# Pairing the first activations with the first weights in the input DMAs of a two-layer encoder kernel

## The chip, the cores and the metric

The kernel runs on one core of a Trainium2 chip. The metric is the device time of one execution in microseconds (us). Work on the core is shared by five engines, each with its own queue that it works through in order: PE (TensorE, matrix products), DVE (VectorE), ACT (ScalarE), POOL (GpSimd) and SP (SyncE, which here only issues DMAs). DMAs move data between the chip's main memory (HBM) and the on-chip memory that the engines read; a DMA's data may be used when all of it has landed.

## The reference

The reference is a hybrid encoder trunk of two layers on 512 tokens of width 1024. Cut to what matters here, a layer is

```python
for i in range(DEPTH):                       # DEPTH = 2
    h = _mixer_sublayer(x, ...)              # begins with proj = x @ w_in[i], 1024 -> 5120 columns
    x = _layer_norm(DEEPNORM_ALPHA * x + h, ln1_g[i], ln1_b[i])
    mlp = jnp.square(jax.nn.relu(x @ w_up[i])) @ w_down[i]
    gate = jax.nn.sigmoid(x @ w_ple_gate[i] + b_ple_gate[i])
    x = _layer_norm(DEEPNORM_ALPHA * x + mlp + gate * (p[i] @ w_ple[i]), ln2_g[i], ln2_b[i])
```

The mixer splits `proj` into queries, keys and values of two kinds of attention (windowed, with shared keys; and dilated in three groups) and into the logits of two gates, and joins the two attentions by those gates. All inputs are float32. What is computed first, and what this case is about, is the product of x with the first columns of `w_in` of layer 0.

## The kernel before

**Precision.** Every large product is made from three: a float32 operand is split into a rounded high part and the rest (`split`, line 248: ACT casts the high part, DVE subtracts it from the source for the low part), and `mm3` (line 306) sums high x high (line 308), x-low x w-high (309) and x-high x w-low (310) in one bank of PSUM. So a tile of x or of weights is usable by PE only after a DMA, an ACT cast and, for the low part, a DVE subtraction.

**Weights.** `plan_layer` lists weight tiles in the order of use, 128 partitions by 1024 columns (512 KB) each; `pack_weights` lays them behind one another in the array `wst`. `fetch` (line 271) issues the DMA of tile c on SP into a buffer `wst` (three buffers in turn); `prep` (line 280) splits it into `whi` and `wlo` (three buffers each as well). A weight in the list `LATER` takes another way, `split_later` (line 252): ACT writes the high part and its negative, and a DMA of POOL adds the source to that (`accum_op`). Tile 5, the first gate's weights `("g", 0, 0)`, is the first of these. `ahead` decides when tiles are fetched and prepared, two ahead of their use.

**The start.** Line 364 to 376 load x, transposed, as eight tiles of 128 rows of contraction by 512 tokens (256 KB each): `xs0` to `xs7`, rows of 2 KB out of `xT`, whose rows are 16 KB long. Tile 0 of the weights is cut into three DMAs of 128, 384 and 512 columns, fetched after `xs0`; tile 1 is fetched after `xs1`, tiles 2 and 3 after `xs7`. The first product, `linear_k_outer` (line 329), runs over contraction outside and over four output blocks m inside: weight tile j holds contraction steps k = 2j and 2j + 1, with four blocks of 128 columns each. For k = 0 it needs `xs0` and columns 0 to 511 of weight tile 0; for k = 1 `xs1` and columns 512 to 1023. Each k is 12 products of PE (four blocks, three products each), 96 in all. Before them PE runs 11 small products (`warm`, line 243) that need no input.

**The channel vectors.** For each layer a DMA of ACT's queue (line 1197) loads 40 columns of biases and norm parameters into `vraw`, and DVE halves 16 of them into `vhalf` (line 1199). The first user of `vhalf` is the first gate.

**What sets the order.** A scheduler orders each engine's queue ahead of time, from the data each instruction needs and an estimate of times; inside `manual_schedule` PE's order is that of the code. A DMA issue of SP also waits until one of eight completion counters is free, so that a ninth DMA waits for the first one to land.

Of the kernel before, what the change touches and what calls it, by code (L numbers as in the profile page):

```python
# [19 lines left out]
SP = mybir.EngineType.SP  # L20

P = 128
S = 512
D = 1024
KT = 8
DEPTH = 2
# [193 lines left out]

def build(nc, tc, plan, down, xT, xN, pT, wst, vec, rows, sink, cst, out):
    ctx = ExitStack()
    PSUM = bass.MemoryType.PSUM
    SWAP = list(range(8, 16)) + list(range(8)) + list(range(16, 32))
    with ctx:
        cp = ctx.enter_context(tc.tile_pool(name="cp", bufs=1))
        wp = ctx.enter_context(tc.tile_pool(name="wp", bufs=3))
# [18 lines left out]
        def split(hi, lo, src):  # L248
            nc.scalar.copy(hi, src)  # L249
            nc.vector.tensor_tensor(lo, src, hi.bitcast(F32), ALU.subtract)  # L250
# [7 lines left out]
        def recent(engine):  # L258
            return next(i for i in reversed(nc.cur_bb.bb.instructions) if i.engine == engine)
# [3 lines left out]
            return tc.issue_after(recent(SP)) if l else ExitStack()  # L263


        offs = np.cumsum([0] + [len(t) * P * P for _, t in plan + down])
        down_at = {key: int(offs[len(plan) + n]) for n, (key, _) in enumerate(down)}
        ready, fetched, held_sets = {}, {}, {}
        at = [0, 0, 0]

        def fetch(c):
            n = len(plan[c][1]) * P
            st = wp.tile([P, 1024], F32, tag="wst", name=f"wst{c}")
            src = wst[int(offs[c]):int(offs[c + 1])].rearrange("(p n) -> p n", p=P)
            cuts = [slice(0, n)] if c else [slice(0, P), slice(P, n // 2), slice(n // 2, n)]
            for a in cuts:
                nc.sync.dma_start(st[:, a], src[:, a])
            fetched[c] = st, cuts

        def prep(c):  # L280
            st, cuts = fetched.pop(c)
            pool, tag, bufs = held_sets.get(plan[c][0][1][0], (wp, "w", 3))
            hi, lo = (pool.tile([P, 1024], F32R, tag=tag + e, name=f"{tag}{e}{c}", bufs=bufs) for e in ("hi", "lo"))
            for a in cuts:
                (split_later if plan[c][0] in LATER else split)(hi[:, a], lo[:, a], st[:, a])
            ready[c] = (hi, lo)

        def ahead(last, further=0):
            while at[1] < len(plan) and at[1] <= max(last, further):
                fetch(at[1])  # L290
                at[1] += 1
                if at[1] - 1 <= last:
                    prep(at[2])
                    at[2] += 1
            while at[2] < len(plan) and at[2] <= last:
                prep(at[2])
                at[2] += 1
# [63 lines left out]
            return pss  # L361


        xhi = cp.tile([P, KT, S], F32R, name="xhi")
# [12 lines left out]


        def attention_block(l, av, rp, vt, OA, OB, begun):
# [813 lines left out]

        for l in range(DEPTH):
            last = l == DEPTH - 1
            vraw = cp.tile([P, 40], F32, tag="vraw", name=f"vraw{l}", bufs=2)
            nc.scalar.dma_start(vraw, vec[l])
# [26 lines left out]
            for u in range(4):  # L1224
                gs = [gate(l, 1, t, vt, np1) for t in (2 * u, 2 * u + 1)]
                w = weights((l, ("bb", u)))
# [4 lines left out]
                for n, g in enumerate(gs):  # L1231
                    t = 2 * u + n
# [313 lines left out]
```

## Time and profile before

| | us |
|---|---|
| three timed runs | 1504.95, 1506.17, 1506.33 (median 1506.17) |
| the profiled execution, its own time | 1504.93 |
| its span, first to last instruction | 1503.2 |
| PE, DVE, ACT, POOL busy | 1491.1, 1044.7, 762.4, 255.1 |
| first large product of PE starts | 4.68 |
| last of the 96 products of the start begins | 27.75 |

The page of the profile gives busy times, the chain that ended last, and the costliest groups; the trace behind it answers with a timeline of each engine. In a timeline a row is: start, duration, engine, line of the kernel, operation, written tile<-read tiles, and in brackets the idle time just before it with what ended it. "SPq", "ACTq" and "POOLq" are DMA issues on those engines' queues.

### The profile page before, as it was taken

What the parts mean: (1) busy time and instruction counts of PE and PEld (TensorE: products, weight loads), DVE (VectorE), ACT (ScalarE), POOL (GpSimd) and SP (SyncE); (2) the same over time, 40 slices, a digit from 0 to 9 for tenths busy, and PEclk for the clock granted to TensorE, in tenths of its full rate; (3) what the DMA queues carried; (4) which work ended last, traced back from release to release, by engine and by line L of the source; (5) the groups of instructions that cost most, each with busy time, mean ns of one, the idle gap of its engine ahead of it and who ended that gap; (6) DMA issues with size and microseconds to landing.
All of it is one profiled execution on the core that took longest, in us unless ns stands there. A gap on an engine that the chain in (4) does not pass through costs nothing.

```text
span 1503.2 us, 19458 instructions
## 1 busy us (share of the span) xinstructions
PE 1491.1 (99%) x7242; PEld 1241.0 (83%) x7242; DVE 1044.7 (69%) x1796; ACT 762.4 (51%) x1256; POOL 255.1 (17%) x216
## 2 busy tenths in 40 slices
PE   9999999999999999999999999999999999999997
PEld 7888888888888888888888888888888888888886
DVE  6766675458577677677877666754685867777778
ACT  5777774344344443434458777643442544444344
POOL 1212211110021110213012122102100202111121
PEclk9999999999999999999999999999999999999999
DMA  7656564555523414142366666546755233241402
GB/s 263 151 135 153 136 160 124 186 160 154 182 60 94 127 57 154 42 141 84 97 203 140 141 148 143 152 135 167 239 153 182 70 113 112 84 127 54 139 18 70
DMA packets 58894, 197.41 MB, mean 131 GB/s; under 512 B 7440, under 2 KB 7984, under 8 KB 58800
## 3 DMA queue, kind: packets, MB, share of 16 engines
q1 hardware_dynamic: 47552, 159.08, 33.1%
q0 software_dynamic: 10256, 36.70, 13.2%
q8 instruction: 56, 0.92, 0.2%
q10 hardware_dynamic: 992, 0.39, 0.1%
q14 instruction: 38, 0.31, 0.1%
HBM read 161.46 MB, written 6.37 MB: 112 GB/s over the span
## 4 chain that ended last, share of the span: by engine, by line
PE 92%; DVE 4%; ACT 1%; DMA 1%; issue 0%; POOL 0%; SPq 0%; DVEq 0%; POOLq 0%; ACTq 0%
PE dn L1156 19%; PE ps_up L310 8%; PE ps_up L309 8%; PE ps_up L308 8%; PE wo L316 2%; PE wo L314 2%; PE wo L315 2%; PE pg L314 2%; PE pg L315 2%; PE pg L316 2%; PE sa L509 1%; PE pta L472 1%; PE sb L504 1%; PE ya L308 1%; PE ya L309 1%; PE ya L310 1%
## 5 line engine op out<-in xcount | busy, mean ns | idle before, releaser
L249 ACT CAST whi<-wst 128x1024 fp32r<-128x1024 f32 (+2 forms) x120 | 121.2, 1010 | 252.2 <-PE ps_up L309 102.7
L250 DVE TENSOR_TENSOR wlo<-wst,whi 128x1024 fp32r<-128x1024 f32 (+2 forms) x120 | 149.2, 1248 | 100.8 <-ACT whi L249 99.6
L1119 POOL TENSOR_TENSOR hr<-r 128x512 f32<-128x512 f32 x64 | 108.8, 1701 | 547.4 <-ACT r L1111 516.1
L310 PE MATMUL ps_up<-xhi,wlo 128*128 128x512 f32 x512 | 199.5, 390 | 0.0
L308 PE MATMUL ps_up<-xhi,whi 128*128 128x512 f32 x512 | 199.4, 390 | 0.0
L309 PE MATMUL ps_up<-xlo,whi 128*128 128x512 f32 x512 | 199.4, 390 | 0.0
L309 PEld LDWEIGHTS ps_up<-xlo,whi 128*128 128x128 f32 x512 | 96.2, 188 | 19.9
L308 PEld LDWEIGHTS ps_up<-xhi,whi 128*128 128x128 f32 x512 | 96.1, 188 | 19.9
L310 PEld LDWEIGHTS ps_up<-xhi,wlo 128*128 128x128 f32 x512 | 96.2, 188 | 19.9
L1172 DVE TENSOR_TENSOR y<-y,dn 128x512 f32<-128x512 f32 (+1 forms) x98 | 65.9, 672 | 62.9 <-PE dn L1156 62.8
L249 ACT CAST whi<-raw 128x1024 fp32r<-128x1024 f32 x56 | 58.0, 1053 | 96.0 <-PE ps_up L309 57.7
L249 ACT CAST dhi<-raw 128x1024 fp32r<-128x1024 f32 x56 | 58.6, 1050 | 85.9 <-PE dn L1156 57.3
L256 POOL DMA_DIRECT2D wlo<-wst x54 | 47.3, 876 | 246.0 <-ACT wlo L255 151.9
L1099 DVE TENSOR_TENSOR raw<-raw,raw 128x1024 f32<-128x1024 f32 x64 | 84.7, 1324 | 0.3
L250 DVE TENSOR_TENSOR wlo<-raw,whi 128x1024 fp32r<-128x1024 f32 x56 | 68.3, 1220 | 14.1 <-ACT whi L249 14.1
L254 ACT CAST whi<-wst 128x1024 fp32r<-128x1024 f32 x54 | 56.5, 1047 | 32.3 <-PE ps_start L309 4.3
L250 DVE TENSOR_TENSOR dlo<-raw,dhi 128x1024 fp32r<-128x1024 f32 x56 | 68.9, 1239 | 3.6 <-ACT dhi L249 3.6
L255 ACT ACTIVATE wlo<-whi 128x1024 fp32r<-128x1024 f32 x54 | 57.3, 1061 | 0.9
L1156 PE MATMUL dn<-wlo,smh 128*128 128x512 f32 (+1 forms) x130 | 51.1, 393 | 0.2
L1130 DVE TENSOR_TENSOR sml<-sr,smh 128x1024 fp32r<-128x1024 f32 x32 | 43.7, 1365 | 10.8 <-ACT smh L1129 10.8
L1156 PE MATMUL dn<-whi,smh 128*128 128x512 f32 (+1 forms) x130 | 50.4, 390 | 0.0
L1156 PE MATMUL dn<-whi,sml 128*128 128x512 f32 (+1 forms) x130 | 50.3, 387 | 0.0
(860 smaller groups left out, 4039.0 us busy)
## 6 DMA issues: line engine op xcount, KB each, us to landing
wst<-wst SPq DMA_DIRECT2D x187, 512.0 KB, 3.6
raw<-wst SPq DMA_DIRECT2D x64, 512.0 KB, 4.3
wlo<-wst POOLq DMA_DIRECT2D x54, 512.0 KB, 5.0
y<-rows POOLq DMA_DIRECT2D x12, 512.0 KB, 7.0
row<-rows SPq DMA_DIRECT2D x7, 512.0 KB, 5.2
R<-line SPq DMA_DIRECT2D x24, 128.0 KB, 3.8
wst<-wst SPq DMA_DIRECT2D x9, 256.0 KB, 2.9
xs<-xT SPq DMA_DIRECT2D x8, 256.0 KB, 6.8
```

What stands on the lines that cost most here:

```text
L249: nc.scalar.copy(hi, src)
L250: nc.vector.tensor_tensor(lo, src, hi.bitcast(F32), ALU.subtract)
L308: nc.tensor.matmul(ps, w[0][:, s], x[0], start=start, stop=False, skip_group_check=part)
L309: nc.tensor.matmul(ps, w[0][:, s], x[1], start=False, stop=False, skip_group_check=part)
L310: nc.tensor.matmul(ps, w[1][:, s], x[0], start=False, stop=stop, skip_group_check=part)
L314: nc.tensor.matmul(ps, x[0], w[0][:, c], start=start, stop=False)
L315: nc.tensor.matmul(ps, x[0], w[1][:, c], start=False, stop=False)
L316: nc.tensor.matmul(ps, x[1], w[0][:, c], start=False, stop=stop)
L1099: nc.vector.tensor_tensor(to, to, other, ALU.add)
L1119: nc.gpsimd.tensor_tensor(h.rearrange("p s t -> p (s t)"), r, r, ALU.mult)
L1156: nc.tensor.matmul(ps, a[:, k, tok], w[b][:, cols], start=first and not (k or m), stop=k == 3 and m == 2, skip_group_check=True)
L1172: return nc.vector.tensor_tensor(to, to, ps, ALU.subtract if n in (2, 4, 5) else ALU.add)
```

## The change

The change touches the start and the place of two small loads; the rest of the program is the same work.

1. The host lays the first six tiles of x and the first three weight tiles side by side. `xw[k]`, for k = 0 to 5, is a block of 128 rows of 4 KB: 2 KB of x tile k, then 2 KB of the four weight blocks of that k. `xw[6]` holds x tiles 6 and 7. Tiles 0 to 2 no longer stand in `wst`.
2. `xw[0]` is loaded by three DMAs (x; 128 columns of weights; 384 columns), `xw[1]` to `xw[6]` by one DMA of 512 KB each. The tiles come from a pool of seven, all of them loaded with no wait for a buffer.
3. The split of the first weights goes in halves of 512 columns, x tile k and the weights of k one after another. For k = 0 DVE, in place of ACT, casts the first 128 columns of the weights.
4. The vectors of both layers come in one DMA, on SP behind the seven, into one tile; they are halved by one instruction.
5. Weight tiles 3, 4 and 5 are now the first to use the three `wst` buffers.

```diff
+FIRST = 3
...
-        offs = np.cumsum([0] + [len(t) * P * P for _, t in plan + down])
+        offs = np.cumsum([0] * (FIRST + 1) + [len(t) * P * P for _, t in (plan + down)[FIRST:]])
...
-            cuts = [slice(0, n)] if c else [slice(0, P), slice(P, n // 2), slice(n // 2, n)]
-            for a in cuts:
-                nc.sync.dma_start(st[:, a], src[:, a])
-            fetched[c] = st, cuts
+            nc.sync.dma_start(st[:, :n], src)
+            fetched[c] = st[:, :n]
...
+        def load_vectors():
+            with tc.issue_after(recent(SP)):
+                nc.sync.dma_start(vraws, vec)
+            nc.vector.tensor_scalar(vhs, vraws[:, :, 0:16], 0.5, None, ALU.mult)
+
...
-        with tc.tile_pool(name="xp", bufs=8) as xp:
-            for k in range(KT):
-                xs = xp.tile([P, S], F32, tag="xs", name=f"xs{k}")
-                nc.sync.dma_start(xs, xT[:, k, :])
-                if k == 0:
-                    ahead(0)
-                split(X[k][0], X[k][1], xs)
-                if k == 1:
-                    ahead(1)
+        with tc.tile_pool(name="xp", bufs=2 * FIRST + 1) as xp:
+            both = [xp.tile([P, 2 * S], F32, tag="xs", name=f"xs{k}") for k in range(2 * FIRST + 1)]
+            for k, st in enumerate(both):
+                for a in ((slice(0, S), slice(S, S + P), slice(S + P, 2 * S)) if not k else (slice(0, 2 * S),)):
+                    nc.sync.dma_start(st[:, a], xw[k][:, a])
+            load_vectors()
+            for k, st in enumerate(both):
+                if k == 2 * FIRST:
+                    for i in range(2):
+                        split(*X[k + i], st[:, i * S:(i + 1) * S])
+                    continue
+                if k % 2 == 0:
+                    ready[k // 2] = [wp.tile([P, 1024], F32R, tag="w" + e, name=f"w{e}{k // 2}", bufs=3) for e in ("hi", "lo")]
+                hi, lo = (t[:, k % 2 * S:(k % 2 + 1) * S] for t in ready[k // 2])
+                own = st[:, S:]
+                if k:
+                    split(*X[k], st[:, :S])
+                    split(hi, lo, own)
+                else:
+                    nc.vector.tensor_copy(hi[:, :P], own[:, :P])
+                    nc.scalar.copy(X[k][0], st[:, :S])
+                    nc.scalar.copy(hi[:, P:], own[:, P:])
+                    nc.vector.tensor_tensor(X[k][1], st[:, :S], X[k][0].bitcast(F32), ALU.subtract)
+                    for a in (slice(0, P), slice(P, S)):
+                        nc.vector.tensor_tensor(lo[:, a], own[:, a], hi[:, a].bitcast(F32), ALU.subtract)
+            at[1] = at[2] = FIRST
...
-            vraw = cp.tile([P, 40], F32, tag="vraw", name=f"vraw{l}", bufs=2)
-            nc.scalar.dma_start(vraw, vec[l])
-            vh = cp.tile([P, 16], F32, tag="vhalf", name=f"vhalf{l}", bufs=2)
-            nc.vector.tensor_scalar(vh, vraw[:, 0:16], 0.5, None, ALU.mult)
+            vraw, vh = vraws[:, l], vhs[:, l]
...
+    xT = np.asarray(x)[0].T.reshape(KT, P, S)
+    first = pack_weights(plan[:FIRST], big).reshape(FIRST, P, 2, S).transpose(0, 2, 1, 3).reshape(2 * FIRST, P, S)
...
+        "xw": np.ascontiguousarray(np.concatenate([np.concatenate([xT[:2 * FIRST], first], axis=2),
+                                                   np.concatenate(xT[2 * FIRST:], axis=1)[None]])),
```

SP's queue at the very start, before (`xs` are the x tiles, `wst0` and `wst1` weight tiles 0 and 1):

```order
L371 DMA xs0_89<-xT 128x512
L277 DMA wst0_91<-wst 128x128
L277 DMA wst0_91<-wst 128x384
L277 DMA wst0_91<-wst 128x512
L371 DMA xs1_105<-xT 128x512
L277 DMA wst1_109<-wst 128x1024
L371 DMA xs2_115<-xT 128x512
L371 DMA xs3_119<-xT 128x512
```

and now (`xs1` and on are the pairs, `vraw` the vectors of both layers, `ct` tables of constants):

```order
L379 DMA xs0_91<-xw 128x512
L379 DMA xs0_91<-xw 128x128
L379 DMA xs0_91<-xw 128x384
L379 DMA xs1_92<-xw 128x1024
L379 DMA xs2_93<-xw 128x1024
L379 DMA xs3_94<-xw 128x1024
L379 DMA xs4_95<-xw 128x1024
L379 DMA xs5_96<-xw 128x1024
L379 DMA xs6_97<-xw 128x1024
L368 DMA vraw_84<-vec 128x80
L276 DMA wst3_199<-wst 128x1024
L411 DMA ct0_166<-cst 128x1920
```

The first three transfers are the same sizes as before; the 512 weight columns and the x tile of k = 1, two DMAs, are one now.

ACT's queue over the same stretch, before, behind its two vector DMAs:

```order
L249 CAST xhi_84<-xs0_89 128x512
L249 CAST whi0_95<-wst0_91 128x128
L249 CAST whi0_95<-wst0_91 128x384
L249 CAST whi0_95<-wst0_91 128x512
L249 CAST xhi_84<-xs1_105 128x512
L249 CAST whi1_111<-wst1_109 128x1024
```

and now:

```order
L395 CAST xhi_86<-xs0_91 128x512
L396 CAST whi0_109<-xs0_91 128x384
L250 CAST xhi_86<-xs1_92 128x512
L250 CAST whi0_109<-xs1_92 128x512
L250 CAST xhi_86<-xs2_93 128x512
L250 CAST whi1_121<-xs2_93 128x512
```

The cast of the first 128 columns has gone to DVE, and for k = 1 the cast of the weights, which stood ahead of that of x, now stands behind it.

POOL's queue at the first gate's weights (`wlo5`, the accumulating DMA), before:

```order
L408 TENSOR_TENSOR swka0_296<-swka0_296,ct0_164 128x512
L408 TENSOR_TENSOR swqa0_0_316<-swqa0_0_316,ct0_164 128x512
L256 DMA wlo5_268<-wst5_265 128x1024
L408 TENSOR_TENSOR swqa0_1_328<-swqa0_1_328,ct0_164 128x512
L429 DMA qh0ka0_302<-qh0ka0_302 64x512
```

and now:

```order
L257 DMA wlo5_264<-wst5_261 128x1024
L432 TENSOR_TENSOR swka0_292<-swka0_292,ct0_166 128x512
L432 TENSOR_TENSOR swqa0_0_312<-swqa0_0_312,ct0_166 128x512
L453 DMA qh0ka0_298<-qh0ka0_298 64x512
L453 DMA qh1ka0_300<-qh1ka0_300 64x512
L432 TENSOR_TENSOR swqa0_1_324<-swqa0_1_324,ct0_166 128x512
```

The accumulating DMA has moved ahead of two rotary products (`swka`, `swqa`) that need results of the 96 products. Past the first score products of layer 0 the queues hold the same instructions in the same order as before.

More of the change, by code (lines that the diff above doesn't have):

```diff
@@ L219, in give, with build @@
         f[f.index(1e9)] = until
-def build(nc, tc, plan, down, xT, xN, pT, wst, vec, rows, sink, cst, out):
+def build(nc, tc, plan, down, xw, xN, pT, wst, vec, rows, sink, cst, out):
     ctx = ExitStack()
@@ L274, in fetch @@
             src = wst[int(offs[c]):int(offs[c + 1])].rearrange("(p n) -> p n", p=P)
-            cuts = [slice(0, n)] if c else [slice(0, P), slice(P, n // 2), slice(n // 2, n)]
-            for a in cuts:
-                nc.sync.dma_start(st[:, a], src[:, a])
-            fetched[c] = st, cuts
+            nc.sync.dma_start(st[:, :n], src)
+            fetched[c] = st[:, :n]
         def prep(c):
-            st, cuts = fetched.pop(c)
+            st = fetched.pop(c)
+            n = st.shape[-1]
             pool, tag, bufs = held_sets.get(plan[c][0][1][0], (wp, "w", 3))
             hi, lo = (pool.tile([P, 1024], F32R, tag=tag + e, name=f"{tag}{e}{c}", bufs=bufs) for e in ("hi", "lo"))
-            for a in cuts:
-                (split_later if plan[c][0] in LATER else split)(hi[:, a], lo[:, a], st[:, a])
+            (split_later if plan[c][0] in LATER else split)(hi[:, :n], lo[:, :n], st)
             ready[c] = (hi, lo)
@@ L361, in start_by_halves @@
             return pss
+        vraws = cp.tile([P, DEPTH, 40], F32, name="vraw")
+        vhs = cp.tile([P, DEPTH, 16], F32, name="vhalf")
+        def load_vectors():
+            with tc.issue_after(recent(SP)):
+                nc.sync.dma_start(vraws, vec)
+            nc.vector.tensor_scalar(vhs, vraws[:, :, 0:16], 0.5, None, ALU.mult)
         xhi = cp.tile([P, KT, S], F32R, name="xhi")
@@ L1524, in cols @@
         return np.asarray(a).reshape(DEPTH, -1, P).transpose(0, 2, 1)
+    xT = np.asarray(x)[0].T.reshape(KT, P, S)
+    first = pack_weights(plan[:FIRST], big).reshape(FIRST, P, 2, S).transpose(0, 2, 1, 3).reshape(2 * FIRST, P, S)
     arrays = {
-        "xT": np.ascontiguousarray(np.asarray(x)[0].T.reshape(KT, P, S).transpose(1, 0, 2)),
+        "xw": np.ascontiguousarray(np.concatenate([np.concatenate([xT[:2 * FIRST], first], axis=2),
+                                                   np.concatenate(xT[2 * FIRST:], axis=1)[None]])),
         "xN": np.ascontiguousarray(np.asarray(x)[0].reshape(4, P, D)),
         "pT": np.ascontiguousarray(np.asarray(p)[:, 0].transpose(0, 2, 1).reshape(DEPTH, 2, P, S).transpose(0, 2, 1, 3)),
-        "wst": pack_weights(plan + down, big),
+        "wst": pack_weights((plan + down)[FIRST:], big),
         "vec": np.ascontiguousarray(np.concatenate(
-            [cols(b_gate), cols(ln1_b), cols(ln2_b), cols(ln2_g)], axis=2)),
+            [cols(b_gate), cols(ln1_b), cols(ln2_b), cols(ln2_g)], axis=2).transpose(1, 0, 2)),
         "rows": np.ascontiguousarray(np.stack([np.asarray(a) for a in (b_ple_gate, ln1_g, ln1_b, ln2_g, ln2_b)], axis=1)),
```

## The prediction

> **What bounds the kernel now.** I read the page first, then the list of PE's waits, then the timelines of PE, ACT, SP and POOL where the change acts. On the page, the row of busy times and the chain that ended last:
>
> ```profile
> PE 1491.1 (99%) x7242; PEld 1241.0 (83%) x7242; DVE 1044.7 (69%) x1796; ACT 762.4 (51%) x1256; POOL 255.1 (17%) x216
> PE 92%; DVE 4%; ACT 1%; DMA 1%; issue 0%; POOL 0%; SPq 0%; DVEq 0%; POOLq 0%; ACTq 0%
> ```
>
> PE is busy for 99% of the span, and the chain runs over it. No product is removed, so what can be won is idle time of PE. All of its listed waits (waiting tile, releaser, us in total, times, longest):
>
> ```profile
> PE out L1426 <- ACT y L1015: 1.5, 1, 1.5
> PE warm L243 <- DVE rgap L239: 1.0, 1, 1.0
> PE ob L513 <- DVE ogb L519: 0.7, 2, 0.4
> PE ps_start L308 <- ACT xhi L249: 0.5, 1, 0.5
> PE dn L1156 <- DVE y L1172: 0.3, 1, 0.3
> PE oa L514 <- DVE ptla L250: 0.3, 2, 0.2
> PE ps_('g', 0, 0)_404 L310 <- DMA wlo<-wst: 0.3, 1, 0.3
> PE xTn L1032 <- DVE y L1019: 0.2, 1, 0.2
> ```
>
> Only two lie where instructions move: `ps_start` (before k = 1 of the first product) and the first gate. The start of PE, as its timeline shows it, and the wait at the gate:
>
> ```profile
> 1.02 3.53 PE L243 MATMUL warm<-rgap 128*88 128x88 f32 x22 [1.02 <-DVE rgap L239]
> 4.68 0.68 PE L308 MATMUL ps_start<-xhi,whi 128*128 128x512 f32 x1
> ...
> 5.94 0.50 PE L308 MATMUL ps_start<-xhi,whi 128*128 128x512 f32 x1
> ...
> 7.43 0.84 PE L310 MATMUL ps_start<-xhi,wlo 128*128 128x512 f32 x3
> 8.76 1.20 PE L308 MATMUL ps_start<-xhi,whi 128*128 128x512 f32 x4 [0.49 <-ACT xhi L249]
> ...
> 27.75 0.39 PE L310 MATMUL ps_start<-xhi,wlo 128*128 128x512 f32 x1
> ...
> 34.11 0.39 PE L309 MATMUL ps_('g', 0, 0)_404<-xlo,whi 128*128 128x512 f32 x1
> 34.81 0.50 PE L310 MATMUL ps_('g', 0, 0)_404<-xhi,wlo 128*128 128x512 f32 x1 [0.31 <-DMA wlo<-wst]
> ```
>
> From the first product of k = 1 (8.76) to the last of the 96 (27.75) there are 83 steps: (27.75 - 8.76) / 83 = 0.229 us a product. So from 8.76 on PE has nothing to win, and the start is decided by one number: **when k = 1 begins**. Twelve products at 0.229 from 4.68 would end at 7.43; k = 1 begins at 8.76. The loss is 1.3 us. What it waits for stands in ACT's timeline (the bracket is the idle time before a row and what ended it):
>
> ```profile
> 0.74 0.90 ACTq L1197 DMA_DIRECT2D vraw<-vec  x2
> 3.81 0.62 ACT L249 CAST xhi<-xs 128x512 fp32r<-128x512 f32 x1 [0.86 <-DMA xs<-xT]
> 4.33 0.29 ACT L249 CAST whi<-wst 128x128 fp32r<-128x128 f32 x1
> 5.37 0.51 ACT L249 CAST whi<-wst 128x384 fp32r<-128x384 f32 x1 [0.74 <-DMA wst<-wst]
> 6.93 0.62 ACT L249 CAST whi<-wst 128x512 fp32r<-128x512 f32 x1 [1.05 <-DMA wst<-wst]
> 8.09 0.62 ACT L249 CAST xhi<-xs 128x512 fp32r<-128x512 f32 x1 [0.54 <-DMA xs<-xT]
> 9.42 1.05 ACT L249 CAST whi<-wst 128x1024 fp32r<-128x1024 f32 x1 [0.71 <-DMA wst<-wst]
> 10.37 2.32 ACT L249 CAST xhi<-xs 128x512 fp32r<-128x512 f32 x4
> 13.12 1.26 ACT L249 CAST xhi<-xs 128x512 fp32r<-128x512 f32 x2 [0.42 <-DMA xs<-xT]
> ```
>
> These give landings: x0 3.8, the 384 columns 5.37, the 512 columns of k = 1 6.93, x1 8.09, weight tile 1 (512 KB of 4 KB rows) 9.42. The transfers set the pace, and they are slow at first (stretch, length, ..., last column GB/s):
>
> ```profile
> 1.75:3.75 2.00, 2.00 (x16) 2.00 (x15) 0.00 (x0) 1.20 (x1) 0.00 (x0) 1.00 0.89 249
> 3.75:8.00 4.25, 4.12 (x18) 2.84 (x16) 2.13 (x6) 1.95 (x4) 0.00 (x0) 1.00 0.90 264
> 9.50:14.00 4.50, 4.50 (x21) 3.64 (x21) 3.50 (x5) 4.02 (x7) 0.00 (x0) 1.00 1.05 405
> ```
>
> **The change part by part.**
>
> *First products of k = 0.* The high x high product of block 0 needs x0's cast and DVE's cast of 128 columns in place of ACT's second one (4.33 to 4.62). No row shows a DVE cast; the nearest is DVE's subtraction of that shape:
>
> ```profile
> 5.07 0.28 DVE L250 TENSOR_TENSOR wlo<-wst,whi 128x128 fp32r<-128x128 f32 x1
> ```
>
> DVE is idle then and runs it beside ACT's 0.62 of x, so the first product comes up to 0.2 us sooner; if the cast took 0.6, nothing. This is worth nothing in the end, since PE's second instruction is now block 1, which needs the 384 columns. That is the real term: before, their cast began at 5.37 and block 1 at 5.94, 0.57 later. The bytes ahead are as before, less the 40 KB of vectors. Bounds for the landing: at worst 5.37 again; at best x0's 3.81 plus 262 KB at 405 GB/s, 4.46. By the stretch's own 249 GB/s it is 3.81 + 1.05 = 4.86, and I take **4.9**. Then block 1 starts at 5.47, eleven products follow each other, and k = 0 ends at 5.47 + 11 x 0.229 = **7.99** (bounds 7.55 and 8.46).
>
> *k = 1.* The 512 columns and x1 come in one DMA; both casts wait for all of it, x first, then weights, 0.62 each, then 0.05 to PE: landing + 1.29. Before, only x1's cast stood behind the last landing, so pairing adds one cast, 0.62. The landing: at worst 8.09, where x1 landed with the same bytes ahead; at best 4.46 + 524 KB at 405 GB/s = 5.75. Tile 1, whose rows are 4 KB like the pair's, came 1.33 after x1; from 4.9 that gives 6.2, and 264 GB/s gives 6.9. I take the middle, **6.5**: k = 1 may begin at 7.8, just under the 7.99 of k = 0. So k = 1 begins at 8.0 and not 8.76: **0.76 us**.
>
> *k = 2 and on.* A pair is 1.3 us of transfer and 1.24 of casts; a step of PE is 12 x 0.229 = 2.75. What is queued only gets further ahead. x6 and x7 land some 6.6 us after the first pair, at 13.1; PE is at k = 6 at 8.0 + 60 x 0.229 = 21.7.
>
> *The vectors.* Two small DMAs leave ACT's queue (0.90 us of issue, ended long before 3.81: nothing on the path), one is added to SP behind the pairs. DVE's halving now waits for it, at about 13.2, and behind it stand the low parts of x6, x7 and tile 3. They are needed from 21.7 on, so the wait is covered by 8 us.
>
> *Tiles 3 to 5.* SP's timeline, and tile 5 on ACT and POOL:
>
> ```profile
> 11.75 0.33 SPq L277 DMA_DIRECT2D wst<-wst  x1
> 12.12 1.50 SPq L1408 DMA_DIRECT2D out<-rows  x2
> 17.37 25.38 SPq L277 DMA_DIRECT2D wst<-wst  x6
> ...
> 24.86 1.05 ACT L254 CAST whi<-wst 128x1024 fp32r<-128x1024 f32 x1 [3.62 <-DMA wst<-wst]
> 27.30 1.07 ACT L255 ACTIVATE wlo<-whi 128x1024 fp32r<-128x1024 f32 x1
> ...
> 28.44 1.21 POOL swqa L408
> 29.65 5.11 DMA wlo<-wst
> ```
>
> Before, tile 5 was issued at 17.37, when the buffer of tile 2 came free, behind two `out` DMAs; it was cast at 24.86, its negative written at 27.30 behind another ACT row, and its accumulating DMA issued on POOL at 29.65 behind `swqa`. It landed at 34.76, and PE stood for it: 34.81 - 34.11 - 0.229 = **0.47 us**. Now tile 5 has a fresh buffer, stands ahead of the `out` DMAs, and its POOL issue ahead of `swka` and `swqa`. What is late next is the buffer of its high part, free when PE has done k = 5, at 21.7: 21.7 + 1.05 + 1.07 + 5.11 = 28.9, against a need at 34.34 - 0.76 = 33.6. The 0.47 goes. The fetches behind it keep their order, and the next accumulating DMA serves a gate that PE reaches 48 products, 11 us, later.
>
> *Sum.* 0.76 + 0.47 = 1.23 us. The profiled execution took 1504.93, and by the sum 1503.7. The timed runs lie at 1504.95, 1506.17 and 1506.33: with the profiled one they are two pairs 1.3 us apart, and the median 1506.17 is in the upper. I subtract from the mean of all four, 1505.6: **1504.4**, which is 0.12% under the median. Less than 0.2% (3.0 us) is about what a measurement of this kernel can tell from no change, so my forecast is a small gain inside that.
>
> **A rule of the skill.** The slow start has row pitch as one possible reason: x rows were 2 KB out of 16 KB. The Trainium skill, "DMA: Bandwidth & Descriptors", section "Latency and other measured facts", says that copies whose row pitch is a large power of two (it lists 512 KiB and more) lose up to half their rate and that contiguous tiles restore it. The trace speaks against it here: behind x1 (8.09) tile 1 and x2 to x7, of the same pitch, 2.1 MB, had landed when the last x cast began at 13.76 (13.12 + 1.26 - 0.62), which is 370 GB/s. By the rule the first pair would land near 5.8 and not 6.5, and as k = 0 decides, the sum stays within 0.1 us.
>
> **The rivals.**
>
> *Everything lands at full rate.* With vectors and long-pitched rows gone, transfers after x0 run at 405 GB/s: 384 columns at 4.46, k = 0 ends 7.55, the pair at 5.75. Gain 8.76 - 7.55 + 0.47 = 1.7 us: 1503.9. If x0 is earlier too, the `warm` row ends it: PE is taken until 4.55, k = 0 ends at 4.55 + 12 x 0.229 = 7.30, gain 1.9. For it: fewer and longer rows. Against: 249 and 264 GB/s with DMA engines 0.9 busy. The same skill page ("Anatomy of one DMA", a fit for DMAs issued from GpSimd) has 2.0 us plus bytes at 436 GB/s; counted from the first issue, 0.74, the pair would land at 5.15, an estimate on this rival's side; x1's landing at 8.09 disagrees.
>
> *Pairing gives back what it saves.* If the pair lands at 7.5, k = 1 begins at 8.79 and only the 0.47 is left: 1505.1.
>
> *Slower: the pair lands late.* With k = 1 bound to the whole 512 KB plus two casts, the start loses once the landing is past 7.47, and the kernel is slower than before past 7.94, when it has eaten the 0.47. If the pair lands where tile 1 did, 9.42, k = 1 begins at 10.71: +1.95 - 0.47 = +1.5, 1507.1. For it: x1 landed at 8.09 with as many bytes ahead. Against: tile 1 was queued beside x1 and was well under way then.
>
> *The 0.47 is not kept.* Attention follows the gate; DVE and ACT work does not come sooner by it. DVE's last row for the first scores and PE's first score product:
>
> ```profile
> 37.98 0.69 DVE L427 TENSOR_TENSOR qlqa<-t1qa,qlqa 64x512 fp32r<-64x512 f32 x1
> ...
> 39.93 0.28 PE L509 MATMUL sa<-qh0ka,qhqa 128*128 128x256 f32 x1
> ```
>
> There is 1.26 us of slack, more than 0.47, though tile 6's split now stands earlier on DVE. If it is lost: 1504.8.
>
> **How the numbers follow.** Chances: forecast 45%, full rate 22%, given back 15%, 0.47 not kept 10%, slower 8%. Low end: the best gain, 1.9, under the lowest run, 1504.95, is 1503.0. High end: the pair at 8.09 is +0.62 - 0.47 = +0.15, on the highest run, 1506.33, 1506.5. The range leaves out the later part of the slower rival and freak runs. Faster by over 0.2% needs less than 1503.2, the best gain on a low run: 6%. Slower by over 0.2% needs 1509.2, beyond even 9.42: 1%. Within: 93%.
>
> **What would show it.** In the new trace: first product of k = 1 at about 8.0 (right), 7.3 to 7.6 (full rate), 8.8 or later (pairing too dear); ACT's first cast out of the first pair at 6.5; no wait of PE at the first gate's low product; the last of the 96 products beginning near 27.0, and attention's first score product near 38.7. A new wait of PE on `xhi`, `xlo` or tiles 3 to 6 after 9 us, or a change of more than 0.3 us anywhere after 60 us, would make the prediction wrong.

## The result, and the profile after

The changed kernel takes 1524.76 us (median of 4 runs, 1523.18 to 1525.21) beside 1505.56 of the kernel before (now 4 runs, the fourth at 1504.67): a ratio of 1.0126, 95% interval 1.0108 to 1.0143. It is 19 us slower. The profiled execution took 1524.55 us, its span 1522.8 (before 1503.2, so 19.6 more). One execution of `before_x128`, a kernel of the experiments below, took 2134.12 us at a granted clock of 0.654 and is left out of its median. The page's row of busy times:

```profile
PE 1510.5 (99%) x7242; PEld 1238.8 (81%) x7242; DVE 1045.5 (69%) x1798; ACT 762.3 (50%) x1257; POOL 250.8 (16%) x216
```

PE was busy for 1491.1 us before and is for 1510.5 now, with the same 7242 products. So the 19 us are no wait; the products themselves take longer. PE's list of waits agrees (waiting tile, releaser, us, times, longest):

```profile
PE out L1447 <- ACT y L1039: 1.5, 1, 1.5
PE warm L244 <- DVE rgap L240: 1.0, 1, 1.0
PE ps_start L307 <- ACT whi L250: 0.9, 1, 0.9
PE ps_start L307 <- ACT whi L396: 0.7, 1, 0.7
PE xTn L1056 <- DVE y L1043: 0.6, 1, 0.6
PE dn L1180 <- DVE y L1196: 0.3, 1, 0.3
PE oa L538 <- DVE ptla L251: 0.3, 2, 0.2
```

At the start, 0.5 became 0.9 + 0.7; the wait at the first gate is gone. That is about 1 us, not 19. ACT and PE at the start, in their timelines:

```profile
3.43 0.62 ACT L395 CAST xhi<-xs 128x512 fp32r<-128x512 f32 x1 [1.41 <-DMA xs<-xw]
5.17 0.51 ACT L396 CAST whi<-xs 128x384 fp32r<-128x384 f32 x1 [1.12 <-DMA xs<-xw]
8.25 0.62 ACT L250 CAST xhi<-xs 128x512 fp32r<-128x512 f32 x1 [2.56 <-DMA xs<-xw]
8.77 0.61 ACT L250 CAST whi<-xs 128x512 fp32r<-128x512 f32 x1
...
5.74 0.97 PE L307 MATMUL ps_start<-xhi,whi 128*128 128x512 f32 x3 [0.70 <-ACT whi L396]
...
9.44 0.50 PE L307 MATMUL ps_start<-xhi,whi 128*128 128x512 f32 x1 [0.87 <-ACT whi L250]
```

The first pair is cast from 8.25 on, and k = 1 begins at 9.44.

Where the rest goes is seen in one stage far from the change: the first quarter of the up projection of layer 0, 192 products `ps_up` in a row, and the stage of down products behind it. From the first product's start to that of the next stage (stretch, length, busy us and count of PE, PEld, DVE, ACT, POOL, granted clock, DMA share, GB/s), before:

```profile
419.26:462.79 43.53, 43.53 (x194) 36.06 (x193) 37.22 (x39) 21.78 (x30) 11.68 (x7) 1.00 0.25 73
462.79:501.30 38.51, 38.48 (x169) 31.39 (x168) 26.02 (x31) 16.28 (x18) 1.04 (x1) 1.00 0.36 109
```

and after:

```profile
424.11:468.91 44.80, 44.80 (x194) 35.91 (x192) 37.42 (x39) 21.79 (x30) 11.34 (x7) 1.00 0.24 71
468.91:507.46 38.55, 38.54 (x169) 31.37 (x168) 25.82 (x30) 16.27 (x18) 1.04 (x1) 1.00 0.36 109
```

(The counts take in products that reach over an edge.) The up stage takes 43.53 / 192 = 226.7 ns a product before and 233.3 after, the down stage the same in both; the clock is 1.00 in all four rows, PE idle in none by more than 0.03 us, and the other engines' work differs by tenths. In a product PE holds one operand, the stationary one, and streams the other past it, 512 columns at a time. Up products stream x past the weights. From the starts of successive products in the trace, the 3504 products that stream a part of x past a stationary weight have steps of 227 ns in the median before and 233 or 234 after, in sum 796.3 and 814.9 us, the waits between them included: **+18.5**. The 384 products of the gate projection that hold x stationary add 0.8, everything else 0.4. The sum, 19.8, is how much later the last product begins; what follows it is 0.2 shorter, and the spans differ by 19.6.

So the question is why a product that streams x takes 6 ns more. The instructions and their order are the same. What differs is an address. The diff in the first part leaves out where the vectors' tiles are allocated; in the pool `cp` they now stand ahead of x's two parts:

```diff
+        vraws = cp.tile([P, DEPTH, 40], F32, name="vraw")
+        vhs = cp.tile([P, DEPTH, 16], F32, name="vhalf")
...
         xhi = cp.tile([P, KT, S], F32R, name="xhi")
         xlo = cp.tile([P, KT, S], F32R, name="xlo")
...
-            vraw = cp.tile([P, 40], F32, tag="vraw", name=f"vraw{l}", bufs=2)
-            vh = cp.tile([P, 16], F32, tag="vhalf", name=f"vhalf{l}", bufs=2)
```

They take 320 + 128 = 448 bytes of each partition. Where the built programs put the tiles (byte in a partition, and that modulo 256):

```
            xhi            xlo            first whi
before      1664   (128)   18048  (128)   47232 (128)
after       2112   (64)    18496  (64)    34944 (128)
```

x moves by 448 bytes, that is by -64 modulo 256. What stands behind x keeps its place modulo 256, since the same 448 bytes stood behind it before; `whi` itself changed places with the buffers of `wst`, by 12288 bytes, which is 48 times 256.

### The profile page after: what moved, and what is told of

It is laid out like the page before. It is cut to its first block, busy times and chain, and to the rows that moved or that the text cites. A ratio compares the mean times of both kernels' runs of the same rounds, so it can differ in the third digit from the quotient of the medians.

```text
span 1522.8 us, 19450 instructions
## 1 busy us (share of the span) xinstructions
PE 1510.5 (99%) x7242; PEld 1238.8 (81%) x7242; DVE 1045.5 (69%) x1798; ACT 762.3 (50%) x1257; POOL 250.8 (16%) x216
## 4 chain that ended last, share of the span: by engine, by line
PE 94%; DVE 3%; ACT 1%; DMA 1%; issue 0%; POOL 0%; SPq 0%; DVEq 0%; POOLq 0%; ACTq 0%
PE dn L1180 18%; PE ps_up L308 8%; PE ps_up L307 8%; PE ps_up L309 8%; PE wo L314 2%; PE wo L315 2%; PE wo L313 2%; PE pg L314 2%; PE pg L315 2%; PE pg L313 2%; PE sa L533 1%; PE sb L528 1%; PE pta L496 1%; PE ya L307 1%; PE ya L308 1%; PE ya L309 1%
## 5 line engine op out<-in xcount | busy, mean ns | idle before, releaser
L250 ACT CAST whi<-wst 128x1024 fp32r<-128x1024 f32 (+1 forms) x115 | 117.3, 1020 | 262.0 <-PE ps_up L308 110.9
L251 DVE TENSOR_TENSOR wlo<-wst,whi 128x1024 fp32r<-128x1024 f32 (+1 forms) x115 | 143.7, 1255 | 107.7 <-ACT whi L250 106.6
L1143 POOL TENSOR_TENSOR hr<-r 128x512 f32<-128x512 f32 x64 | 105.5, 1648 | 561.7 <-ACT r L1135 531.1
L314 PE MATMUL pg<-blo,xhi 128*128 128x512 f32 x128 | 50.3, 393 | 0.0
```

Source lines behind the costliest of these rows:

```text
L314: nc.tensor.matmul(ps, x[0], w[1][:, c], start=False, stop=False)
L1143: nc.gpsimd.tensor_tensor(h.rearrange("p s t -> p (s t)"), r, r, ALU.mult)
```

## Experiments

**First theory:** the address of x, not the new loading, makes its products slow. The rival is the new loading itself. `x_first` is the changed kernel with x's parts allocated first again:

```diff
+        xhi = cp.tile([P, KT, S], F32R, name="xhi")
+        xlo = cp.tile([P, KT, S], F32R, name="xlo")
         vraws = cp.tile([P, DEPTH, 40], F32, name="vraw")
         vhs = cp.tile([P, DEPTH, 16], F32, name="vhalf")
...
-        xhi = cp.tile([P, KT, S], F32R, name="xhi")
-        xlo = cp.tile([P, KT, S], F32R, name="xlo")
```

> The changed kernel, with one thing undone: x's high and low parts are allocated ahead of the vector tiles, so that they stand at byte 1664 of a partition again and not at 2112. Same instructions, DMAs and queues as the changed kernel. Placement theory (products that stream x pay for an address that is not a multiple of 128): steps of these products go back from 233 to 227 ns, the 3504 of them give back about 18.6 us, and the time is 1505.6 plus what the start itself is worth, which the trace puts between -0.3 and +0.7: 1505 to 1506.5. Start theory (the new loads, their layout or buffers slow the products): it stays near 1524.8. If only the slow start mattered: 1524.

Measured: 1505.28 us (11 runs, 1504.23 to 1506.13), ratio to the kernel before 0.9996 (0.9987 to 1.0005). All 19 us are back, with every DMA and cast of the change in place. The up stage in its windows, and rows of its timeline on ACT and PE:

```profile
419.36:462.88 43.52, 43.52 (x193) 36.05 (x192) 37.22 (x39) 21.78 (x30) 11.68 (x7) 1.00 0.23 73
...
5.26 0.51 ACT L395 CAST whi<-xs 128x384 fp32r<-128x384 f32 x1 [1.27 <-DMA xs<-xw]
8.09 0.62 ACT L250 CAST xhi<-xs 128x512 fp32r<-128x512 f32 x1 [2.32 <-DMA xs<-xw]
...
9.29 1.19 PE L307 MATMUL ps_start<-xhi,whi 128*128 128x512 f32 x4 [0.69 <-ACT whi L250]
...
34.82 0.39 PE L309 MATMUL ps_('g', 0, 0)_400<-xhi,wlo 128*128 128x512 f32 x1
```

This run also shows the change's intended effect alone. k = 1 begins at 9.29, 0.53 later than before (8.76); the gate's low product, which waited before, begins at 34.82 beside 34.81. The start loses what the gate gains, and the change is worth nothing.

**Which property of the address?** The first theory took the operand's own address: good at a multiple of 128, bad at 64 past one. Three kernels put it to the test on the kernel before, with small unused tiles (`pada` ahead of x, `padb` between its parts, `padc` behind them):

```diff
+        pada = cp.tile([P, 16], F32, name="pada")
+        nc.gpsimd.memset(pada, 0.0)
         xhi = cp.tile([P, KT, S], F32R, name="xhi")
         xlo = cp.tile([P, KT, S], F32R, name="xlo")
+        padc = cp.tile([P, 16], F32, name="padc")
+        nc.gpsimd.memset(padc, 0.0)
```

That is `before_x64`. `before_x128` has a `pada` of 128 bytes and no other, `before_xlo64` a `padb` of 64 and a `padc` of 64. All three also shift everything behind x in that pool and the weights by 128.

> The kernel before, with a tile of 64 bytes put ahead of x's parts and one of 64 bytes behind them: x stands at 1728 (64 past a multiple of 128), all that follows moves by 128. Loads and order as before, two small memsets on POOL added. Placement theory: the same 233 ns a step as the changed kernel, 1505.6 + 19 = 1524.5. Start theory: 1505.6.

> The kernel before, with a tile of 128 bytes ahead of x's parts: x at 1792, again a multiple of 128, what follows moves by 128 as in the run with 64. Placement by multiples of 128: 227 ns, 1505.6. If any move away from 1664 costs (a bank, a distance to another tile): about 1524. Start theory: 1505.6.

> The kernel before, with 64 bytes between x's high and low parts and 64 behind: only the low part is 64 past a multiple of 128. One product in three streams the low part (line 309 in the kernel before). Placement theory, cost borne by the tile that is streamed: only those steps go from 227 to 233, so 1168 x 5.3 ns = 6.2 us, 1511.8. If the distance between the two parts or the pool's layout as a whole were at work: all three kinds alike, 1524 or 1505.6.

Measured: 1534.07 us (ratio 1.0191, 1.0177 to 1.0205), 1516.78 (1.0075, 1.0059 to 1.0090) and 1528.0 (1.0149, 1.0135 to 1.0163). All three are slower, and the first theory misses. The windows of the same up stage and the down stage behind it, of `before_x64`:

```profile
425.81:470.61 44.80, 44.80 (x194) 35.95 (x192) 37.42 (x39) 21.78 (x30) 11.34 (x7) 1.00 0.23 71
470.61:509.95 39.34, 39.31 (x170) 31.61 (x169) 26.10 (x30) 16.25 (x18) 1.04 (x1) 1.00 0.35 107
```

of `before_x128`:

```profile
422.00:465.55 43.55, 43.55 (x194) 36.07 (x193) 37.22 (x39) 21.80 (x30) 11.69 (x7) 1.00 0.23 73
465.55:504.89 39.34, 39.32 (x170) 31.60 (x168) 26.30 (x31) 16.25 (x18) 1.04 (x1) 1.00 0.34 107
```

and of `before_xlo64`:

```profile
423.75:468.12 44.37, 44.37 (x193) 36.06 (x192) 37.43 (x39) 21.78 (x30) 11.24 (x7) 1.00 0.23 72
468.12:507.45 39.33, 39.31 (x169) 31.60 (x168) 26.09 (x30) 16.25 (x18) 1.04 (x1) 1.00 0.35 107
```

In the last, the products xhi x whi, xlo x whi and xhi x wlo step by 228, 233 and 232 ns in the median, though the operands of the first and the third stand at the same places modulo 256.

The down stage is the key. Its products hold the activations stationary (`smh` and its like) and stream the weights. It went from 38.51 to 39.34, although its stationary operand had not moved (`smh` stands at byte 179840, 128 modulo 256, in these as in the kernel before). The weights that it streams had, to 0 modulo 256, a multiple of 128, which the first theory calls good. In `before_x128` x moved with the weights, and the up stage stayed at 43.55. So what counts is **how far apart the two operands stand**, and that was the second theory: a product is at its shortest where streamed and stationary operand have the same address modulo 256. Its rival is an address of one of them by itself.

Three kernels move the weights alone: the kernel before with one unused tile of 64, 128 or 256 bytes behind x (`[P, 16]`, `[P, 32]`, `[P, 64]`):

```diff
         xlo = cp.tile([P, KT, S], F32R, name="xlo")
+        pad = cp.tile([P, 16], F32, name="pad")
+        nc.gpsimd.memset(pad, 0.0)
```

and a fourth is the slow changed kernel with 192 bytes there, which leaves x where it is and moves the weights to x's place modulo 256:

```diff
         xlo = cp.tile([P, KT, S], F32R, name="xlo")
+        pad = cp.tile([P, 48], F32, name="pad")
+        nc.gpsimd.memset(pad, 0.0)
```

> The kernel before with 64 bytes put behind x's parts: x stays at 1664, the weight tiles and all that is allocated behind them move by 64. Absolute theory (a streamed operand must stand at a multiple of 128): x still does, so its products stay at 227 ns; products that stream a weight tile would slow down. Relative theory (what counts is the distance between the streamed operand and the weights that PE loads meanwhile, modulo 256: 0 is free): x and weights are 64 apart, 233 ns for all products of x; the down projection, whose other operand stands still at the far end, slows as well; about 1505.5 + 19 + 11 = 1535.

> The kernel before with 128 bytes behind x's parts: x at 1664, weights moved by 128, both multiples of 128. Absolute theory by 128: 1505.5. Relative theory modulo 256: x and weights 128 apart, products of x at about 232 (as the down projection's 231.5 in the run with x and weights moved by 128 together), 1505.5 + 11 + about 17 = 1533.

> The kernel before with 256 bytes behind x's parts: distances change by 256. Relative theory modulo 256: 227 ns for every kind, 1505.5. If the distance counts modulo 512 or more: as slow as with 128, about 1533. Absolute theory by 128: 1505.5.

> The changed kernel with x left at 2112 (64 past a multiple of 128) and 192 bytes put behind it, so that x and the weight tiles are again a multiple of 256 apart. Relative theory: the products of x go back to 227 ns although x's own address is what it was in the slow kernel; the down projection, whose other operand has not moved, goes to about 231.5, as when the weights moved by 128: about 1505.5 + 11 = 1517 or somewhat more. Absolute theory: products of x stay at 233, 1524 or more.

Measured: 1530.27 us (ratio 1.0162, 1.0132 to 1.0191), 1529.61 (1.0157, 1.0128 to 1.0187), 1505.55 (1.0000, 0.9989 to 1.0012) and 1514.48 (1.0064, 1.0041 to 1.0087). The two stages of `before_w64`:

```profile
424.75:469.54 44.79, 44.79 (x193) 36.09 (x192) 37.44 (x39) 21.77 (x30) 11.38 (x7) 1.00 0.24 71
469.54:508.38 38.84, 38.78 (x169) 31.43 (x168) 25.91 (x30) 16.27 (x18) 1.04 (x1) 1.00 0.35 108
```

of `before_w256`:

```profile
418.88:462.39 43.51, 43.51 (x193) 36.03 (x192) 37.21 (x39) 21.78 (x30) 11.67 (x7) 1.00 0.25 73
462.39:500.89 38.50, 38.49 (x169) 31.38 (x168) 26.02 (x31) 16.29 (x18) 1.04 (x1) 1.00 0.34 109
```

and of `after_w192`:

```profile
419.94:463.51 43.57, 43.57 (x194) 36.04 (x193) 37.22 (x39) 21.77 (x30) 11.68 (x7) 1.00 0.23 73
463.51:502.98 39.47, 39.45 (x169) 31.50 (x168) 26.32 (x31) 16.29 (x18) 1.04 (x1) 1.00 0.35 107
```

`after_w192` settles it: x stands at byte 2112 as in the slow kernel, the weights have moved to 64 modulo 256 as well, and the up stage is back from 44.80 to 43.57 us. Its down stage pays instead, since `smh` stayed at 128. And 256 bytes make no difference, so the modulus is 256. All stages beside the distances that the programs' addresses give (streamed minus stationary operand, modulo 256). In the up stage (192 products) x is streamed, in the down stage (168) the weights are:

```
              up: distance           us        down: distance    us
before               0             43.53              0        38.51
before_x128          0             43.55            128        39.34
before_w256          0             43.51              0        38.50
after_w192           0             43.57            192        39.47
x_first              0             43.52              0        38.52
before_w128        128             44.63            128        39.47
after              192             44.80              0        38.55
before_x64         192             44.80            128        39.34
before_w64         192             44.79             64        38.84
before_xlo64   128 (xhi), 192 (xlo) 44.37           128        39.33
```

The down column follows the same order: 2.0 ns a product at 64, 4.9 to 5.7 at 128, 5.7 at 192. It also shows that the distance has a direction. In `before_w64` the weights stand 64 bytes further on. For the up stage, where they are stationary, this is a distance of 192, 6.6 ns a product; for the down stage, where they are streamed, it is 64. The expected 1535 us had counted the down products as at 128 (+11 us); 1530 were measured.

**Is it PE alone?** A rival was left: that the loss needs DVE, ACT or DMAs at the same memory. `distances` runs nothing but products, with rows such as

```diff
+            group("w0x0", 0, 0)
+            group("w0x64", 0, 64)
...
+            group("w64x64", 64, 64)
```

> A kernel of products alone; all the rest of the reference is left out, and its output is a copy of some input. Fifteen groups of 96 products of 128x512 (128x256 in two of them), each with another pair of distances from a common base at which stationary and streamed operand have the same address modulo 256: wAxB has the stationary operand A bytes on and the streamed one B bytes on. Nothing else runs beside them. Theory (the distance of the two operands modulo 256 sets the step, within PE): w0x0, w0x256, w64x64 and w128x128 step by 227 ns, w0x64, w0x128, w0x192 and w64x0 by 232 to 233, which is 21.8 and 22.3 us for a group; w0x16, w0x32 and w0x96 show from which distance on. In the group mixed (distances 128, 192, 128 in turn, the pattern of before_xlo64) the products at 128 that follow one another differ, as hh and hl did there, 228 against 232. Rival (the loss needs other engines or DMAs that use the memory at the same time): all groups of 512 columns step by 227, whatever the distance.

Measured in one execution, in the windows of its groups, 96 products each. In order: w0x0, w0x64, w0x128, w0x192, w0x256, w64x64, w64x0, w128x128:

```profile
30.53:52.29 21.76, 21.76 (x97) 18.02 (x96) 0.00 (x0) 0.00 (x0) 0.00 (x0) 1.00 0.00 0
52.29:74.28 21.99, 21.99 (x97) 18.03 (x96) 0.00 (x0) 0.00 (x0) 0.00 (x0) 1.00 0.00 1
74.28:96.59 22.31, 22.31 (x97) 18.09 (x96) 0.00 (x0) 0.00 (x0) 0.00 (x0) 1.00 0.00 1
96.59:118.99 22.40, 22.40 (x97) 17.95 (x96) 0.00 (x0) 0.00 (x0) 0.00 (x0) 1.00 0.00 1
118.99:140.77 21.78, 21.78 (x98) 18.02 (x96) 0.00 (x0) 0.00 (x0) 0.00 (x0) 1.00 0.00 0
140.77:162.57 21.80, 21.80 (x97) 18.02 (x96) 0.00 (x0) 0.00 (x0) 0.00 (x0) 1.00 0.00 1
162.57:184.97 22.40, 22.40 (x98) 17.95 (x97) 0.00 (x0) 0.00 (x0) 0.00 (x0) 1.00 0.00 1
184.97:206.78 21.81, 21.81 (x98) 18.02 (x96) 0.00 (x0) 0.00 (x0) 0.00 (x0) 1.00 0.00 1
```

The rival falls: with every other engine idle and the DMAs moving next to nothing, 96 products take 21.8 us at equal addresses modulo 256, wherever these are, and up to 22.40 at others, 226.7 and 233.3 ns a product. One number was expected otherwise: 64 bytes cost only 2.4 ns, not 5 to 6. The group that repeats `before_xlo64`'s pattern repeats its odd result, 228, 233 and 232 ns for the three products of a turn; so that too is PE's own. Of the other groups, the streamed operand 16, 32 and 96 bytes on took 22.24, 22.41 and 22.40 us. Products of 256 columns took 11.51 us at distance 0 and 11.31 at 64: for them distance 0 is no gain.

**Which access?** PEld, the load of the stationary operand, is busy for 18.0 of those 21.8 us, beside the streaming. The third theory was that the next product's load collides with it. `which_access` shifts single operands and narrows the loads.

> Products alone again, all the rest of the reference left out; groups of 96 products, 512 columns streamed, nothing beside them. xall_a to xall_i: every streamed operand 0, 32, 64 and so on to 256 bytes on. wfourth and weighth: only every fourth or eighth stationary operand is 64 bytes on; xfourth and xeighth: only every fourth or eighth streamed operand is 192 bytes on. half and quarter: 64 and 32 stationary columns in place of 128, at 0 (a) and 192 (g). short: bfloat16 operands at 0, 64, 128 and 192. Theory (the load of the next product's stationary operand collides with the streaming of this one): in weighth one step of eight is long, that of the product ahead of the shifted one, by 6 ns; in xeighth the step of the shifted product itself; half and quarter lose a half and a quarter of the 6.6 ns a product; xall_a and xall_i step by 227, all between by 229 to 234. Rival (the distance of a product's own two operands matters): the long step in weighth is that of the shifted product itself, and half and quarter lose as much as the whole. For bfloat16 neither says anything; a loss of 0 or of some ns is possible.

Some of its groups in the timeline of one execution (start, duration of 96 products): the streamed operand 0, 32, 64, 192 and 256 bytes on, then 64 and 32 stationary columns at distance 0 and at 192, and at last bfloat16 operands at 0 and 192:

```profile
32.09 21.92 PE L40 MATMUL xall_a<-xa,wa 128*128 128x512 f32 x96
53.85 22.57 PE L40 MATMUL xall_b<-xa,wa 128*128 128x512 f32 x96
76.25 22.15 PE L40 MATMUL xall_c<-xa,wa 128*128 128x512 f32 x96
...
165.53 22.55 PE L40 MATMUL xall_g<-xa,wa 128*128 128x512 f32 x96
...
210.31 21.93 PE L40 MATMUL xall_i<-xa,wa 128*128 128x512 f32 x96
...
320.53 22.24 PE L40 MATMUL half_a<-xa,wa 128*64 128x512 f32 x96
342.61 22.50 PE L40 MATMUL half_g<-xa,wa 128*64 128x512 f32 x96
364.94 22.39 PE L40 MATMUL quarter_a<-xa,wa 128*32 128x512 f32 x96
387.17 22.40 PE L40 MATMUL quarter_g<-xa,wa 128*32 128x512 f32 x96
409.42 20.89 PE L40 MATMUL short_a<-xc,wb 128*128 128x512 bf16 x94
...
471.58 20.88 PE L40 MATMUL short_g<-xc,wb 128*128 128x512 bf16 x94
```

The steps are as expected from 0 to 256. The third theory isn't borne out, and neither is its rival. With one stationary operand in eight shifted (`weighth`), the step ahead of the shifted product stays at 226 ns, its own is 235.7, and the three behind it take 228.3, 232.7 and 230.7 before it settles at 226.7: a disturbance that runs on, so a product's own distance does not settle its step. 64 columns lose 0.26 us a group at 192 and 32 columns 0.01, where a half and a quarter of the 0.63 of 128 columns were expected; and both are slower already at distance 0 (22.24 and 22.39 beside 21.92). Which two accesses meet stays open. bfloat16 operands show no effect of the distance.

**Can the change be made to pay?** In `x_first` both casts of k = 1 stand behind one landing. `x_first_split` loads that pair by two DMAs, weights first, and casts each as it lands:

```diff
-                for a in ((slice(0, S), slice(S, S + P), slice(S + P, 2 * S)) if not k else (slice(0, 2 * S),)):
+                for a in ((slice(0, S), slice(S, S + P), slice(S + P, 2 * S)), (slice(S, 2 * S), slice(0, S)))[k] if k < 2 else (slice(0, 2 * S),):
...
+                if k == 1:
+                    split(hi, lo, own)
+                    split(*X[k], st[:, :S])
```

> The changed kernel with x's parts allocated ahead of the vectors (as in x_first) and, besides, the pair of k = 1 loaded by two DMAs of 512 columns, weights first and x second, with the weights cast by ACT as they land. Theory (the start term was lost because a pair is one landing: both casts of k = 1 stand behind the landing of all 512 KB): the weights are cast before x lands, so k = 1 begins one cast after x's landing, 8.1 + 0.62 + 0.06 = about 8.8 us in place of the 9.25 of x_first, and the time is 0.5 us below x_first's: 1504.8. Rival (the landing itself is later when the pair is two DMAs of 2 KB rows, so that nothing is gained): k = 1 still begins at 9.2 or later, 1505.3. All steps of the large products stay at 227 ns under both.

ACT and PE in its timeline:

```profile
6.85 0.62 ACT L250 CAST whi<-xs 128x512 fp32r<-128x512 f32 x1 [0.85 <-DMA xs<-xw]
7.49 0.62 ACT L250 CAST xhi<-xs 128x512 fp32r<-128x512 f32 x1
...
8.66 1.07 PE L307 MATMUL ps_start<-xhi,whi 128*128 128x512 f32 x4
...
34.06 0.39 PE L309 MATMUL ps_('g', 0, 0)_401<-xhi,wlo 128*128 128x512 f32 x1
```

The mechanism holds: k = 1 begins at 8.66 with no wait, the cast of x follows that of the weights at once, and the gate's low product is reached at 34.06, 0.75 us earlier than before. The time can't show that: 1505.54 us (11 runs) beside 1505.68 (27 runs), ratio 1.0002 (0.9993 to 1.0011), an interval of 1.4 us to either side.

**Does the distance explain the other long steps?** In the kernel before, 635 steps take 230 to 260 ns, many of them in products of gates, queries, keys and values, with attention products between them; they lie 4.2 us in sum over 227 each. The attention tiles stand at 192 modulo 256, x and the weights at 128. `before_attn192` moves them:

```diff
+            gap = av.tile([P, 48], F32, tag="gap", name=f"gap{l}", bufs=1)
+            nc.gpsimd.memset(gap, 0.0)
```

> The kernel before with a gap of 192 bytes in the pool of the attention tiles, so that these begin 128 bytes past a multiple of 256, as x and the weights do, and no longer 192 past it. Theory (distance of the two operands modulo 256): products that stand beside attention products, where the one reads operands at 128 and the next at 192, now take 231 to 236 ns; all steps between 215 and 260 ns of the kernel before lie 2.1 us in sum above 227 each, and most of this goes: 1503.5 to 1504.5. Rival (the longer steps there come from the change between products of different shapes, not from addresses): 1505.5, and the steps stay at 231 to 236.

Measured: 1505.37 us (11 runs), ratio 1.0001 (0.9992 to 1.0009), and as many such steps (639 and 635) with the same sum (4.1 and 4.2 us). The theory misses there; those steps have another reason, which wasn't looked for.

`split_attn` has both edits:

> Both edits together: x's parts ahead of the vectors, the pair of k = 1 as two DMAs, the attention tiles 192 bytes on. If both theories hold, their gains add: 0.5 of the start and 1 to 2 of the attention, 1503 to 1504, ratio to the kernel before 0.998 to 0.999. If neither holds: 1505.3, as x_first. If only the start gains: 1504.8.

Measured: 1506.2 us (11 runs), ratio 1.0003 (0.9994 to 1.0012). No version beats the kernel before by an amount that can be told.

## Why the prediction was wrong

**The step that failed** is the one on the vectors. It priced their move by queues: 0.90 us of issue off ACT, one DMA on SP, a wait of DVE "covered by 8 us". PE's list shows no wait by any of these, but the move has a second part that the sum counted at nothing without naming it: 448 bytes of two tiles now stand ahead of x, and every product that streams x then takes 233 ns and not 227. That is +18.5 us, fifteen times the whole forecast gain and of the other sign; no rival had it, and "slower by over 0.2%" had 1%. The condition at the end of the prediction, a change of more than 0.3 us after 60 us, is what came true: the up stage alone, at 420 us, differs by 1.27 us. "No product is removed, so what can be won is idle time of PE" read a busy time as fixed. It is fixed only while the operands' places are.

**The start term**, 0.76 us to be won, was -0.53 (`x_first`: k = 1 at 9.29, not 8.0; in the changed kernel 9.44). Two landings were mis-sized. The 384 columns were put at 4.9 and were cast from 5.26 on (`x_first`) and 5.17 (after). The pair was put at 6.5 and came at 8.09 and 8.25, at and just past the bound named as the worst one: as late as x1 before, though 40 KB less stood ahead of it and its rows were 4 KB. Loaded as two DMAs, the same pair was there by 7.49 (`x_first_split`) and by 6.94 (`split_attn`); what bounds the pace up to there no run here names. The formula was right to 0.1 us: landing + 1.29 gives 9.38 and 9.54, measured 9.29 and 9.44. Pairing adds a cast, as the step said.

**The gate term**, 0.47 us, was right: the wait is gone from the list, and in `x_first` the 0.53 lost at the start is 0.01 at the gate.

**Sum without the addresses:** -0.53 + 0.47 is a loss of 0.06 us, and `x_first` measures 0.9996. The rival "the pair lands late" had its price for this landing, +0.15 at 8.09, and its deciding point, 7.94, right to 0.1 us. Had it been the forecast, it would still have missed 19 us.

**k = 2 and on** was right: ACT's pairs keep ahead of PE, and after 9.4 no wait on `xhi` or `xlo` shows.

## What to carry to other kernels

When a change adds, moves or resizes a tile in a pool, list the addresses of the big products' operands before and after, and which of the two is streamed. For float32r products of 128x512 on this chip, keep streamed and stationary operand equal modulo 256 bytes; pad the small tiles, or put them behind the large ones. When a span grows and PE's busy time grows with it, compare one stage far from the change at equal counts and clock before looking for waits.

## What the runs showed of the hardware

The step of a float32r product of 512 columns depends on the distance of its operands (streamed minus stationary) modulo 256 bytes: 226.7 ns at 0, 229.0 at 64, 232.4 to 233.3 at 128, 233.3 at 192 and at 32 (windows of `distances`, rows of `which_access`, from the start of one group to that of the next). In whole kernels this made 9 to 29 us of 1505. It needs no other engine, does not depend on either address by itself, and was not seen with bfloat16 operands or with float32r products of 256 columns. Which two accesses meet is open: in a sequence of mixed distances two products of the same distance differ, 228 and 232 ns.

The Trainium skill, "SBUF — State Buffer", section "SBUF: two separate sides", says of the engines against one another that "PE, ACT, and DVE's dedicated pair never wait on anyone", and its section "A bandwidth-pool intuition that's wrong (but worth ruling out)" gives PE a second, independent read port for loading weights. By a second port that is wholly independent the place of the weights would not matter to the streaming; with PE alone at work, w0x0 took 21.76 us and w64x0 22.40, so the measurement decides: PE's two operands do affect one another.

A pair of 512 KB issued as one DMA of 4 KB rows was there at 8.09 us (`x_first`) and at 8.25 (the changed kernel); as two DMAs of 2 KB rows its second half was there by 7.49 (`x_first_split`) and by 6.94 (`split_attn`). One profile of each shows this, and why it is so was not tested.
